# Nine matmuls behind the heads' products read their columns in other orders, by a word for each of fourteen units

## Chip, cores and metric

The kernel runs on one core of a Trainium2 chip. The metric is the device time of one execution in microseconds, the median of several runs. Before the change it is 1700.52 us (three runs, 1699.19 to 1701.03).

## What is computed

One decoder layer on 256 rows of 4096 float32 numbers: an RMS norm, a projection to q, k, v and gate of 32 heads, stick-breaking attention, a second projection that is added to the input, and a last RMS norm.

```python
xn = rms_norm(x, norm_attn)
q, k, v, g = split(xn @ w_in, 4)              # w_in: 4096 x 16384
# per head, strictly causal (s < t):
log_a[t, s] = log_sigmoid(z[t, s]) + sum_{s < j < t} log_sigmoid(-z[t, j]),  z = q k^T / sqrt(128)
o = exp(log_a) @ v
h = x + (o * silu(g)) @ w_out                 # w_out: 4096 x 4096
out = rms_norm(h, final_norm)
```

## The kernel before

**Arithmetic.** Both factors of a large product are split into a high part and a rest (`h` and `l`, both float32r), and a product is the sum of three matmuls: high by high, high by rest, rest by high. Each has 128 rows, 128 stationary columns and 512 moving columns, and adds into one PSUM bank. `mm3` (line 813) issues the three. The moving operand is a slice of a weight tile (`wh`, `wl`), the stationary one a block of the input (`sh`, `sl`; in the second projection `oh`, `ol`).

**Units.** The work is cut into 20 units: units 0 to 15 take the columns of `w_in` that give two heads each, units 16 to 19 the columns of `w_out`. A unit has 16 steps, each over 256 of the 4096 rows of the contraction. From unit 1 on, a step has seven or eight products (a Strassen form in some steps, the plain form with two shared sums in the others), so 21 or 24 matmuls. Seven PSUM banks gather a unit's products (`acc`), the eighth (`att`) serves the heads.

**Heads.** While the products of unit u run, the two heads of unit u-1 are worked off. Each head has four groups of small products on TensorE: the transposes (`tr`), the scores (`z`), the scan that sums the logs (`z` again) and the weighted values (`o`). So a unit u from 2 to 15 has eight such groups among its big products. `ten` (line 345) gives a group to the planner with an earlier key than any big product, so that it is next on TensorE as soon as its inputs are there.

**Who sets the order.** `Plan` is an event-driven planner with a cost for each instruction. It emits the instructions of all engines in one order. TensorE takes them in that order, ScalarE makes the high parts `wh`, VectorE the rests `wl` and, at a unit's end, adds up the banks (`combine`), SyncE loads the weights as `raw`, GpSimd issues loads that add.

**Order of reading.** A matmul's 512 columns may be read in any order, if the output is written in the same one. `mm3` rearranges both by two numbers q and e: the 512 columns are cut into pieces of q*e, and the matmul makes q rounds, in each of which it takes the next run of e columns from every piece. A letter names the order: `e` is 4 rounds in runs of 8, `c` is 4 rounds in runs of 4. A word of three letters belongs to a product, one letter to each of its matmuls. `product` (line 1234) chooses the word: `since_others` counts the big products since the last group of a head, and the first seven take the words of `BEHIND_OTHERS` (line 37): `ccc ecc eee eee eee eee cce`. Later the first product of a step takes one of `IN_STEP`, and every other product is `eee`.

Of the kernel before, what the change touches and what calls it, by code (L numbers as in the profile page):

```python
# [31 lines left out]
NS = KC // KT  # L32
EPS = 1e-6

ROUNDS = 4
RUNS = {"e": 8, "c": 4}
BEHIND_OTHERS = ("ccc", "ecc", "eee", "eee", "eee", "eee", "cce")
IN_STEP = ("cce", "ecc")
WARM, IDLE = 10, 640


# [207 lines left out]
def kernel(  # L249
# [61 lines left out]
    for g, (n, k) in enumerate(order):  # L311
        p = parts[n]
# [30 lines left out]
    since_others = 0  # L343
# [469 lines left out]
    def mm3(out_, a, b, start, stop, orders):  # L813

        (ah, al), (bh, bl) = a, b
        for k, (x, y) in enumerate(((ah, bh), (ah, bl), (al, bh))):
            to, y = (t.rearrange("p (h q e) -> p q h e", q=ROUNDS, e=RUNS[orders[k]]) for t in (out_, y))
            nc.tensor.matmul(to, x, y, start=start and k == 0, stop=stop and k == 2, skip_group_check=True)


# [413 lines left out]
    def product(n, k):  # L1234
        nonlocal since_others
        p = parts[n]
        b, f, c = p["prods"][k]
        h, l = forms[p["s"]]
        orders = "eee"
        if since_others < len(BEHIND_OTHERS):  # L1240
            orders = BEHIND_OTHERS[since_others]
        elif p["i"] == 0 and k == 0:
            orders = IN_STEP[p["s"] % len(IN_STEP)]
        since_others += 1
        mm3(
            ev[p["u"]][b],
            (h[:, PLACES[f], :], l[:, PLACES[f], :]),
            tuple(t[:, c].rearrange("p i n -> p (i n)") for t in (wh[n], wl[n])),
            starts[p["u"], b] == (n, k),
            ends[p["u"], b] == (n, k),  # L1250
            orders,
        )

    def products():
        for g, (n, k) in enumerate(order):
            p = parts[n]
            u, s = p["u"], p["s"]
            b, f, c = p["prods"][k]
            if u < 1:
                what = "s"  # L1260
            elif u < OUT0:
                what = "n"
            elif u == OUT0:
                what = "o"
            else:
                what = "r" if u == LAST and s in EIGHT_LAST else "p"
            if starts[u, b] == (n, k):
                yield nc.take(f"b{b}")
                ev.setdefault(u, {})[b] = acc.tile([P, W], F32, tag=f"b{b}", name=f"acc{u}_{b}")
            yield nc.until(("low", n, c), ("form", what, s), lead=nc.LEAD)  # L1270
            yield nc.work(
                "tensor", PRODUCT, lambda: product(n, k), g * PRODUCT, after=lambda n=n, k=k: done(n, k), hold=False
            )
            nc.here = g * PRODUCT
# [59 lines left out]
```

## Time and profile before

| | |
|---|---|
| median of three runs | 1700.52 us |
| the profiled execution | 1698.9 us |
| its span, first to last instruction | 1697.1 us |
| TensorE, granted clock | 0.997 |
| big matmuls, all units | 7158 |

The profiled execution is 1.8 us longer than its span, and 1.6 us shorter than the median. The profile names one line for every instruction, because all are recorded in one helper; tiles tell them apart. In the timeline each row has the start, the duration, the engine and the tiles (output<-operands); a matmul's duration is that of its whole way through the array, so it is the distance between two starts that tells how fast TensorE goes on.

### The profile page before, as it was taken

How to read it: one execution, taken by the hardware profiler on the slowest of the kernel's cores; microseconds unless marked ns; L12 is line 12 of the kernel's file. 1: busy time of each engine (PE TensorE's matmuls, PEld its weight loads, DVE VectorE, ACT ScalarE, POOL GpSimd, SP SyncE). 2: the span in 40 equal slices, each digit the busy share in tenths (PEclk: the TensorE clock that was granted, in tenths of full speed). 3: DMA queues.
4: the chain of work that ended last, by engine and by line, in shares of the span. 5: the costliest groups of instructions: out<-in, count | busy, mean ns of one | idle time of the engine just before them, and what ended most of it. 6: DMA issues, size and time to landing. Idle time of an engine off the chain costs nothing.

```text
span 1697.1 us, 25128 instructions
## 1 busy us (share of the span) xinstructions
PE 1680.2 (99%) x7776; PEld 1417.4 (84%) x7776; DVE 1602.0 (94%) x2025; ACT 1206.7 (71%) x1665; POOL 324.9 (19%) x400
## 2 busy tenths in 40 slices
PE   9999999999999999999999999999999999999997
PEld 7888888888888888888888888888888888888885
DVE  8899999999999999999999999999999978999997
ACT  8986767676767676767676767676868775656654
POOL 0012222121222222222212121212122111212110
PEclk9999999999999999999999999999999999999998
DMA  9978888878787878797978797979797978888895
GB/s 343 332 197 247 232 247 222 252 217 253 215 256 212 256 212 266 199 272 196 276 201 269 198 268 196 272 198 269 204 264 210 300 230 266 245 245 256 246 304 185
DMA packets 248438, 412.77 MB, mean 243 GB/s; under 512 B 28016, under 2 KB 72560, under 8 KB 248304
## 3 DMA queue, kind: packets, MB, share of 16 engines
q1 hardware_dynamic: 194544, 354.24, 62.7%
q0 software_dynamic: 53472, 56.65, 20.0%
q8 instruction: 61, 1.00, 0.2%
q14 instruction: 73, 0.60, 0.1%
q10 hardware_dynamic: 288, 0.28, 0.1%
HBM read 402.93 MB, written 8.13 MB: 242 GB/s over the span
## 4 chain that ended last, share of the span: by engine, by line
PE 94%; DVE 3%; DMA 1%; issue 1%; ACT 1%; SPq 0%; DVEq 0%; ACTq 0%
PE acc L132 89%; PE z L132 3%; PE o L132 1%; DVE wl L132 1%; PE tr L132 1%; DVE h L132 1%; DVE raw L132 0%; ACT wh L132 0%; DMA raw<-in_w_out_dram 0%; DMA raw<-in_w_in_dram 0%; DMA xres<-in_x_dram 0%; SPq L132 0%; ACT sq L132 0%; DVE scalars L132 0%; DVE qk_sb L132 0%
## 5 line engine op out<-in xcount | busy, mean ns | idle before, releaser
L132 ACT CAST wh<-raw 128x1024 fp32r<-128x1024 f32 (+1 forms) x989 | 919.3, 970 | 385.5 <-DVE raw L132 160.9
L132 DVE TENSOR_TENSOR wl<-raw,wh 128x1024 fp32r<-128x1024 f32 (+1 forms) x815 | 975.7, 1220 | 49.3 <-ACT wh L132 23.9
L132 PE MATMUL acc<-wh,sh 128*128 128x512 f32 x2048 | 771.9, 389 | 0.1
L132 PE MATMUL acc<-wh,sl 128*128 128x512 f32 x1898 | 727.1, 383 | 1.8 <-DVE sl L132 1.8
L132 PE MATMUL acc<-wl,sh 128*128 128x512 f32 x1748 | 668.9, 383 | 0.1
L132 PEld LDWEIGHTS acc<-wh,sh 128*128 128x128 f32 x2048 | 384.0, 188 | 77.9 <-DVE qk_sb L132 4.9
L132 POOL DMA_DIRECT2D raw<-in_w_in_dram x300 | 258.3, 947 | 972.2 <-DMA raw<-in_w_in_dram 375.1
L132 PEld LDWEIGHTS acc<-wh,sl 128*128 128x128 f32 x1898 | 356.0, 188 | 66.3 <-DVE sl L132 2.4
L132 PEld LDWEIGHTS acc<-wl,sh 128*128 128x128 f32 x1748 | 328.4, 188 | 55.6 <-DVE wl L132 0.4
L132 DVE TENSOR_TENSOR raw<-raw,raw 128x512 f32<-128x512 f32 x348 | 238.3, 688 | 15.3 <-DMA raw<-in_w_in_dram 11.7
L132 PE MATMUL acc<-wh,oh 128*128 128x512 f32 x512 | 192.4, 383 | 0.0
L132 PE MATMUL acc<-wh,ol 128*128 128x512 f32 x488 | 186.7, 383 | 0.0
L132 PE MATMUL acc<-wl,oh 128*128 128x512 f32 x464 | 177.6, 383 | 1.4 <-DVE wl L132 1.4
L132 DVE TENSOR_TENSOR wh<-raw,wh 128x512 fp32r<-128x512 f32 x174 | 119.7, 688 | 3.3 <-ACT wh L132 2.7
L132 DVE TENSOR_TENSOR raw<-raw 128x512 f32<-128x512 f32 x174 | 119.4, 686 | 0.0
L132 PEld LDWEIGHTS acc<-wh,oh 128*128 128x128 f32 x512 | 96.1, 188 | 17.3
L132 PEld LDWEIGHTS acc<-wh,ol 128*128 128x128 f32 x488 | 91.5, 188 | 16.1
L132 PEld LDWEIGHTS acc<-wl,oh 128*128 128x128 f32 x464 | 87.1, 188 | 17.6 <-DVE wl L132 2.2
L132 POOL DMA_DIRECT2D raw<-in_w_out_dram x48 | 41.5, 984 | 173.8 <-DMA raw<-in_w_out_dram 85.2
L132 ACT ACTIVATE f<-f 128x384 f32<-128x384 f32 x96 | 50.5, 526 | 3.0
L132 POOL DMA_DIRECT2D p<-spill x27 | 17.0, 676 | 89.9 <-DVE ol L132 32.0
L132 DVE SCALAR_TENSOR_TENSOR gv_sb<-acc,scalars,gv_sb 128x512 f32<-128x512 f32 x45 | 33.5, 745 | 0.0
(86 smaller groups left out, 765.7 us busy)
## 6 DMA issues: line engine op xcount, KB each, us to landing
raw<-in_w_in_dram SPq DMA_DIRECT2D x1024, 256.0 KB, 4.5
raw<-in_w_out_dram SPq DMA_DIRECT2D x256, 256.0 KB, 4.5
raw<-in_w_in_dram POOLq DMA_DIRECT2D x300, 128.0 KB, 5.2
p<-spill POOLq DMA_DIRECT2D x27, 256.0 KB, 4.6
raw<-in_w_out_dram POOLq DMA_DIRECT2D x48, 128.0 KB, 5.4
xr<-in_x_dram SPq DMA_DIRECT2D x16, 256.0 KB, 5.3
xres<-in_x_dram SPq DMA_DIRECT2D x16, 256.0 KB, 5.5
out_dram<-h SPq DMA_DIRECT2D x16, 256.0 KB, 2.8
```

The lines of the kernel that those rows point to most:

```text
L132: return self.tc.keep_in_program_order(getattr(self.engine, name)(*args, **kw))
```

## The change

Two more orders get a letter: `g` is 2 rounds in runs of 8, and `r` reads the 512 columns as they lie. In units 2 to 15 the first three products behind each group of a head take their three words from a table by unit, in place of `ccc ecc eee`; the fourth to seventh stay as they are, and so do all other units.

```diff
-ROUNDS = 4
-RUNS = {"e": 8, "c": 4}
+RUNS = {"e": (4, 8), "c": (4, 4), "g": (2, 8), "r": (1, 512)}
 BEHIND_OTHERS = ("ccc", "ecc", "eee", "eee", "eee", "eee", "cce")
 IN_STEP = ("cce", "ecc")
+BY_UNIT = (
+    "cec eee eee", "cce eee eee", "ecc eee eee", "cce ccc eee", "ecc ece eee", "gcc eee eee", "ece cec ccc",
+    "eee eec cee", "ece eee eee", "ccc cee eee", "eee eee eee", "ccr eee eee", "cec cec eee", "ecc ccc eee",
+)
...
-            to, y = (t.rearrange("p (h q e) -> p q h e", q=ROUNDS, e=RUNS[orders[k]]) for t in (out_, y))
+            q, e = RUNS[orders[k]]
+            to, y = (t.rearrange("p (h q e) -> p q h e", q=q, e=e) for t in (out_, y)) if q > 1 else (out_, y)
...
             orders = BEHIND_OTHERS[since_others]
+            if 2 <= p["u"] < 2 + len(BY_UNIT) and since_others < 3:
+                orders = BY_UNIT[p["u"] - 2].split()[since_others]
```

No instruction is added, removed or moved on any engine, and no wait changes. 384 of the 7158 big matmuls get another order: 296 go from `c` to `e`, 72 from `e` to `c`, 8 from `c` to `g` and 8 from `c` to `r`.

On TensorE in unit 12, behind the transposes of the second head of unit 11, there stood (128x4x32x4 is order `c`, 128x4x16x8 order `e`; the name behind the arrow is the moving tile, then the stationary one):

```order
L132 MATMUL tr11_1_10144<-ident_129,qk_sb11_9832 128x128 x4
L132 MATMUL acc12_3_9963<-wh617_10004,sh4_279 128x4x32x4 x2
L132 MATMUL acc12_3_9963<-wh617_10004,sl4_280 128x4x32x4
L132 MATMUL acc12_7_9998<-wh618_10034,sh4_279 128x4x16x8
L132 MATMUL acc12_7_9998<-wl618_10124,sh4_279 128x4x32x4
L132 MATMUL acc12_7_9998<-wh618_10034,sl4_280 128x4x32x4
L132 MATMUL acc12_5_9944<-wh618_10034,sh4_279 128x4x16x8
```

and now there stands, with the word `eee eee eee` of unit 12:

```order
L135 MATMUL tr11_1_10144<-ident_129,qk_sb11_9832 128x128 x4
L135 MATMUL acc12_3_9963<-wh617_10004,sh4_279 128x4x16x8 x2
L135 MATMUL acc12_3_9963<-wh617_10004,sl4_280 128x4x16x8
L135 MATMUL acc12_7_9998<-wh618_10034,sh4_279 128x4x16x8
L135 MATMUL acc12_7_9998<-wl618_10124,sh4_279 128x4x16x8
L135 MATMUL acc12_7_9998<-wh618_10034,sl4_280 128x4x16x8
L135 MATMUL acc12_5_9944<-wh618_10034,sh4_279 128x4x16x8
```

The same matmuls stand in the same places; all five that were in order `c` are in order `e`.

On TensorE in unit 8, behind the scores of the second head of unit 7, there stood:

```order
L132 MATMUL z7_1_6980<-off_139,ident_b_140 128x256
L132 MATMUL acc8_1_6777<-wh412_6865,sh5_325 128x4x32x4
L132 MATMUL acc8_1_6777<-wl412_6876,sh5_325 128x4x32x4
L132 MATMUL acc8_1_6777<-wh412_6865,sl5_326 128x4x32x4
L132 MATMUL acc8_2_6710<-wh412_6865,sh5_325 128x4x16x8
L132 MATMUL acc8_2_6710<-wl412_6876,sh5_325 128x4x32x4
L132 MATMUL acc8_2_6710<-wh412_6865,sl5_326 128x4x32x4
L132 MATMUL acc8_3_6759<-wh413_6850,sh5_325 128x4x16x8 x2
L132 MATMUL acc8_3_6759<-wh413_6850,sl5_326 128x4x16x8
```

and now, with the word `ece cec ccc` of unit 8:

```order
L135 MATMUL z7_1_6980<-off_139,ident_b_140 128x256
L135 MATMUL acc8_1_6777<-wh412_6865,sh5_325 128x4x16x8
L135 MATMUL acc8_1_6777<-wl412_6876,sh5_325 128x4x32x4
L135 MATMUL acc8_1_6777<-wh412_6865,sl5_326 128x4x16x8
L135 MATMUL acc8_2_6710<-wh412_6865,sh5_325 128x4x32x4
L135 MATMUL acc8_2_6710<-wl412_6876,sh5_325 128x4x16x8
L135 MATMUL acc8_2_6710<-wh412_6865,sl5_326 128x4x32x4
L135 MATMUL acc8_3_6759<-wh413_6850,sh5_325 128x4x32x4 x2
L135 MATMUL acc8_3_6759<-wh413_6850,sl5_326 128x4x32x4
```

Again only the orders differ: seven of the nine have changed, and the third product, which had none in order `c`, has all three.

## The prediction

> **What bounds the kernel now.** I read the page first: the busy time of each engine against the span.
>
> ```profile
> span 1697.1 us, 25128 instructions
> ...
> PE 1680.2 (99%) x7776; PEld 1417.4 (84%) x7776; DVE 1602.0 (94%) x2025; ACT 1206.7 (71%) x1665; POOL 324.9 (19%) x400
> ```
>
> TensorE is busy for 99% of the span, VectorE for 94%. Then one unit alone, from the table of stretches (length, then TensorE, weight loads, VectorE and so on):
>
> ```profile
> 599.00:683.00 84.00, 84.00 (x393) 70.94 (x393) 81.33 (x98) 61.12 (x81) 17.73 (x21) 1.00 0.83 235
> ```
>
> Within this steady unit TensorE has no gap, and its granted clock is 1.00. VectorE is busy for 81.33 of 84.00 us, so it could follow a TensorE that were 2.7 us faster in a unit. What TensorE does wait for, the list of waits shows:
>
> ```profile
> PEld acc L132 <- DVE qk_sb L132: 4.9, 14, 0.5
> PEld acc L132 <- PE acc L132: 4.7, 14, 0.3
> ```
>
> Each comes 14 times, once at each turn from one unit to the next: a bank of the old unit must be added up by VectorE before the new one may use it (the second row blames a matmul; the timeline has VectorE's `gv_sb` add ending there). Together they are (4.9 + 4.7) / 14 = 0.69 us for each unit. Apart from them a steady unit's time is the sum of the distances between starts on TensorE. The change touches nothing but the order in which 384 matmuls read, so it can act only through these distances, and I read them from the timeline of TensorE.
>
> **What the old words cost.** Behind the transposes of the second head in unit 6 (the first row holds the first two big matmuls, the second the tenth, the third the fifteenth):
>
> ```profile
> 537.89 0.69 PE L132 MATMUL acc<-wh,sh 128*128 128x512 f32 x2
> ...
> 539.98 0.38 PE L132 MATMUL acc<-wh,sh 128*128 128x512 f32 x1
> ...
> 541.08 0.38 PE L132 MATMUL acc<-wh,sl 128*128 128x512 f32 x1
> ```
>
> From the tenth to the fifteenth are five distances in 1.10 us: 0.220 us each. This is the quiet pace, in order `e`. From the first to the tenth are nine distances in 2.09 us, where the quiet pace would give 1.98: **0.11 us too long**. I call this the excess of a group. Behind the scores of the same head:
>
> ```profile
> 541.99 0.47 PE L132 MATMUL acc<-wh,sh 128*128 128x512 f32 x1
> ...
> 543.89 0.39 PE L132 MATMUL acc<-wh,sl 128*128 128x512 f32 x1
> 544.12 0.38 PE L132 MATMUL acc<-wh,sh 128*128 128x512 f32 x1
> ```
>
> Nine distances in 2.13 us: excess 0.15. The last of them, 0.23 us, is between two matmuls in order `e`, so the same order goes at two paces: the quiet one, and a slow one that an interruption leaves behind and that ends at some later point. Behind the scan and behind the values of that head (first and tenth matmul of each):
>
> ```profile
> 550.01 0.47 PE L132 MATMUL acc<-wh,sh 128*128 128x512 f32 x1
> ...
> 552.14 0.38 PE L132 MATMUL acc<-wh,sh 128*128 128x512 f32 x1
> ...
> 554.13 0.47 PE L132 MATMUL acc<-wh,sh 128*128 128x512 f32 x1
> ...
> 556.23 0.38 PE L132 MATMUL acc<-wh,sh 128*128 128x512 f32 x1
> ```
>
> The excesses are 0.15 and 0.12. The mean of the four is (0.11 + 0.15 + 0.15 + 0.12) / 4 = **0.13 us with `ccc ecc eee`**. I take it for seven of the eight groups of a unit; the first one is apart, below.
>
> **What words without a pair of `c` cost.** No group of a head is followed by another word in this trace, so I take the nearest rows: matmuls in order `e` behind another interruption, a wait. In unit 0 (interrupted matmul, the next one, and the tenth behind the wait's end):
>
> ```profile
> 10.12 0.50 PE L132 MATMUL acc<-wh,sl 128*128 128x512 f32 x1 [1.75 <-DVE sl L132]
> 10.45 0.40 PE L132 MATMUL acc<-wh,sh 128*128 128x512 f32 x1
> ...
> 12.53 0.40 PE L132 MATMUL acc<-wh,sh 128*128 128x512 f32 x1
> ```
>
> The restart itself takes 0.33 us, 0.11 too long. The nine distances behind it take 2.08 us, 0.10 too long, or 0.011 each, and the slow pace has not ended when the next `ccc` comes at 12.53. And in unit 17 (first and eleventh matmul behind a wait, all in order `e`):
>
> ```profile
> 1515.60 0.50 PE L132 MATMUL acc<-wl,oh 128*128 128x512 f32 x1 [0.29 <-DVE wl L132]
> ...
> 1518.07 0.39 PE L132 MATMUL acc<-wh,ol 128*128 128x512 f32 x1
> ```
>
> Ten distances in 2.47 us: 0.27 too long. So ten distances in order `e` cost 0.21 to 0.27, which I take as **0.24, or 0.11 more than the old words**. If the pace then stays slow until the seventh product's `cce`, up to nine more matmuls pay 0.011 each. From the starts above, the scores are followed by (550.01 - 541.99) / 0.22, over 30 matmuls, the scan by (554.13 - 550.01) / 0.22, under 19, so I add a mean of 0.06. An `e` word costs 0.11 + 0.06 = 0.17 us a group more, seven groups 1.2 us a unit. The ends are 0, if order `e` behind a group gets quiet as soon as the old words do, and 7 x (0.27 - 0.13 + 0.10) = 1.7 us.
>
> **What one pair of `c` costs.** In the first group of a unit the transposes are followed by one product, then the wait on VectorE of 0.3 us, then a product in `ecc` and one in `eee`, up to the scores. That is a pair of `c` behind an interruption with no second pair. In unit 6 (first matmul behind the wait, and the scores, six matmuls later):
>
> ```profile
> 516.52 0.47 PE L132 MATMUL acc<-wh,sh 128*128 128x512 f32 x1
> ...
> 517.97 0.82 PE L132 MATMUL z<-qkT 128*128 128x128 f32 x4
> ```
>
> and the same place in unit 7:
>
> ```profile
> 600.77 0.46 PE L132 MATMUL acc<-wh,sh 128*128 128x512 f32 x1
> ...
> 602.18 0.38 PE L132 MATMUL z<-qkT 128*128 128x128 f32 x2
> ```
>
> 1.45 and 1.41 us for six distances of 0.22 (1.32): excesses 0.13 and 0.09. In unit 7 the pair ended the slow pace, in unit 6 it did not (both last distances are rounded to 0.01). With four more matmuls, quiet or at 0.011, a group would have 0.09 or 0.17; the mean, 0.13, is that of the old words. So **one pair at the front is worth as much as the old two**, on the mean: 0 us, with 0.04 either way.
>
> **The sum.** Units by word:
> - A pair of `c` in the first product (units 3, 4, 5, 6, 7, 11, 13, 15): 0. This puts `gcc` and `ccr` with the others; `g` and `r` stand in no big matmul of this trace, and 16 matmuls are too few to matter unless they spoil the pair beside them, at most 7 x 0.17 = 1.2 us in each of the two units.
> - No two `c` side by side in all nine (units 2, 10, 12): `eee eee eee` 1.2 us. `cec` and `ece` hold single ones; between 0 and 1.2, I take the middle, 0.6 each. Together 2.4 us.
> - Two `c` side by side, but late: `cec cec` at the third and fourth matmul (unit 14), `ece cec ccc` at the sixth (unit 8), `eec cee` there too (unit 9). Until then each matmul pays 0.011 more: 7 x 0.02, 7 x 0.06 and 7 x 0.07, together 1.0 us.
> - The first group of each unit: its first product lies beside the wait on VectorE, which ends when VectorE is done, so a slower or faster word there costs nothing as long as the wait of 0.3 us is left. In the product behind the wait, `eee` takes the place of `ecc` in units 2, 3, 4, 7, 10, 12 and 13: 0.11 + 5 x 0.011 = 0.165 against the mean of 0.13 and 0.09, or 0.05 more, seven times: 0.4 us.
>
> 2.4 + 1.0 + 0.4 = **3.8 us longer**. The profiled execution of 1698.9 us would become 1702.7; the median was 1700.5, which gives **1704.3 us**. A difference of 0.2%, 3.4 us, is about what a measurement of this kernel can tell from no change, so the forecast lies just beyond it.
>
> **The rivals.**
> 1. *The orders settle nothing.* The slow pace ends by itself after a while, and pairs of `c` only shift when. Then words cost what they cost now: 1700.5, at most 1 us off. For it: in the rows behind the scores the pace is slow at the tenth matmul in spite of two pairs. Against it: at 10.45 it lasted nine matmuls without a `c` and more. The Trainium skill goes further in "TensorE: Matmul & The Clock Gate", section "Back-to-back issue gap": the gap depends on the number of columns alone, which for 512 warm columns is 216 ns. By that no word could cost anything, and the time would stay 1700.5. The trace does not agree: the same 512 columns go at 220 and at 230 ns.
> 2. *Faster: the second pair was waste.* If one pair always ends the slow pace, as in unit 7, a group falls from 0.13 to 0.09. In the eight units with a pair at the front that is 8 x 7 x 0.04 = 2.2 us; if the single `c` do as well, in all fourteen units 3.9 us: 1696.6 to 1698.3. It decides from the point at which more than nine in ten groups lock at the first pair; unit 6 speaks against that.
> 3. *Slower by much: only the old words lock.* Every new word behaves as order `e`: 14 x 1.2 = 16.8 us, 1717. If half of them do, 1709. Against it: unit 7.
> 4. *VectorE gives it back.* A unit that takes longer lets VectorE, with 2.7 us free, get ahead, and the 0.69 us of waiting at the turn shrinks. Then units 2, 10, 12 keep at most 0.5 us of their 1.2 and the sum is under 1 us: 1701.3. Against it is the row
>
> ```profile
> ACT wh L132 <- PE acc L132: 148.7, 106, 4.5
> ```
>
> ScalarE waits 106 times for TensorE to free a tile, and VectorE's rests come behind ScalarE's high parts, so both are mostly paced by TensorE and come later with it.
>
> **How the numbers follow.** Chances: the forecast, 2 to 7 us longer, 50%; rival 1, 17%; rival 2, 13%; rival 3 beyond 7 us, 10%; rival 4, 10%. The forecast's lower end, 2 to 3.4 us, is within 0.2% and has 8 of its 50; rival 2 reaches beyond -3.4 us only if nearly every group locks, 5 of its 13, and I add 1 for what I do not see. That gives faster 6%, same 42%, slower 52%. The range of 8 in 10 leaves out the far half of rival 2 and the far part of rival 3: from 1698.5 to 1709. Its upper end is half the bound of rival 3, its lower end half the bound of rival 2.
>
> **What would show it.** In the profile after, the same places by the same reading: in unit 12 nine distances behind a group take 2.2 us or more, in unit 2 and 10 between that and the old 2.11, in units 3, 4, 5, 15 some groups 2.07 and others 2.15, as before on the mean. The length of unit 12 should be about 1 us over that of unit 15. The two waits at the turn should still be 0.3 to 0.5 us; if they shrink, rival 4 holds. If unit 12 is as long as before, the price of order `e` behind a group was wrong, and with it the sum; if units 3 and 4 are the ones that grew, the pair at the front was. No other engine's work should change.

## The result and the profile after

The changed kernel takes **1704.86 us** (median of six runs, 1704.20 to 1706.13), the kernel before 1700.30 in as many: the ratio is 1.0033, with a 95% interval of 1.0023 to 1.0043. It is slower by 4.6 us, and the interval begins just above 0.2%.

The page after, again first the span and the busy times:

```profile
span 1702.9 us, 25128 instructions
...
PE 1686.2 (99%) x7776; PEld 1417.7 (83%) x7776; DVE 1604.1 (94%) x2025; ACT 1208.2 (71%) x1665; POOL 324.8 (19%) x400
```

The span is 5.8 us longer than before, TensorE is busy for 6.0 us more with the same instructions, and VectorE for 2.1. The longest of the fourteen units, unit 5, in the table of stretches:

```profile
431.20:516.10 84.90, 84.90 (x393) 71.03 (x393) 81.43 (x98) 61.11 (x83) 17.38 (x22) 1.00 0.83 232
```

TensorE is still without a gap and its granted clock is still 1.00, so the added 0.8 us of this unit is in the distances between matmuls. The waits at the turn of a unit are in sum as they were (4.9 and 4.7 before):

```profile
PEld acc L135 <- DVE qk_sb L135: 4.8, 14, 0.4
PEld acc L135 <- PE acc L135: 4.7, 14, 0.3
```

Unit 6 again, with the word `ecc ece eee`: first and tenth matmul behind the transposes, the scores, the scan and the values of the second head, and of the last group the twenty-second too:

```profile
541.02 0.47 PE L135 MATMUL acc<-wh,sh 128*128 128x512 f32 x1
...
543.13 0.39 PE L135 MATMUL acc<-wh,sh 128*128 128x512 f32 x1
...
545.19 0.47 PE L135 MATMUL acc<-wh,sh 128*128 128x512 f32 x1
...
547.29 0.38 PE L135 MATMUL acc<-wh,sh 128*128 128x512 f32 x1
...
553.17 0.48 PE L135 MATMUL acc<-wh,sh 128*128 128x512 f32 x1
...
555.33 0.39 PE L135 MATMUL acc<-wh,sh 128*128 128x512 f32 x1
...
557.39 0.47 PE L135 MATMUL acc<-wh,sh 128*128 128x512 f32 x1
...
559.53 0.39 PE L135 MATMUL acc<-wh,sh 128*128 128x512 f32 x1
...
562.28 0.39 PE L135 MATMUL acc<-wh,sh 128*128 128x512 f32 x1
```

The excesses over nine quiet distances (1.98) are 0.13, 0.12, 0.18 and 0.16; before they were 0.11, 0.15, 0.15 and 0.12. That is only 0.06 more in all. The last two rows show where more is lost: from the tenth to the twenty-second matmul are twelve distances in 2.75 us, where twelve quiet ones take 2.64. Before, the same stretch (556.23 to the row below) took 2.64:

```profile
558.87 0.38 PE L132 MATMUL acc<-wh,sh 128*128 128x512 f32 x1
```

Lined up matmul by matmul, the two traces give each unit's length, from its first big matmul to that of the next unit. The differences, with the prices that the prediction put on the words (what it put on the first groups, 0.05 in seven units, is not in the column):

| unit | word | priced | after - before, us |
|---|---|---|---|
| 2 | cec eee eee | 0.6 | +0.48 |
| 3 | cce eee eee | 0 | +0.78 |
| 4 | ecc eee eee | 0 | +0.39 |
| 5 | cce ccc eee | 0 | +0.84 |
| 6 | ecc ece eee | 0 | +0.45 |
| 7 | gcc eee eee | 0 | -0.22 |
| 8 | ece cec ccc | 0.4 | +0.30 |
| 9 | eee eec cee | 0.5 | -0.02 |
| 10 | ece eee eee | 0.6 | +0.51 |
| 11 | ccc cee eee | 0 | +0.36 |
| 12 | eee eee eee | 1.2 | +0.61 |
| 13 | ccr eee eee | 0 | +0.29 |
| 14 | cec cec eee | 0.1 | +0.13 |
| 15 | ecc ccc eee | 0 | +0.23 |

Together +5.13 us. By place behind a group: +0.79 us in the first nine distances, **+3.95 in the tenth to the twenty-first**, +0.39 later. So three quarters are lost among matmuls whose order did not change. The rest of the 5.8 us lies where no word changed: the first big matmul starts 0.75 us later in its trace than before, unit 0 is 0.22 shorter, and units 16 to 19 are together 0.09 longer (17 is 0.29 shorter, 18 0.61 longer).

Two rows of the table are not the words' alone. At the turn into unit 7 the profile before has a longer wait than at any other turn:

```profile
598.76 0.19 PEld L132 LDWEIGHTS acc<-wh,sh 128*128 128x128 f32 x1 [0.50 <-DVE qk_sb L132]
```

From the last matmul ahead of it to this start are 0.47 us; in the change it is 0.31, as at the other turns before. So 0.17 of the 0.22 us that unit 7 gained are a shorter wait, and `gcc` itself gained 0.05. All differences of unit 7 below have this 0.17 us in them. In unit 8 of the change the wait is the longer one, by 0.09 us.

A count of groups shows the mechanism. Take the seven groups behind the first of each of the fourteen units, 98 in all, and call a group still slow if the two distances behind its tenth matmul are together more than 8 ns too long. Before, 0 of 98 are still slow; in the change 55 are, 33 of them among the 56 groups with a pair at the front.

### The profile page after: what moved, and what is told of

It reads as the page before. It is cut to its first block, busy times and chain, and to the rows that moved or that the text cites. A ratio compares the mean times of both kernels' runs of the same rounds, so it can differ in the third digit from the quotient of the medians.

```text
span 1702.9 us, 25128 instructions
## 1 busy us (share of the span) xinstructions
PE 1686.2 (99%) x7776; PEld 1417.7 (83%) x7776; DVE 1604.1 (94%) x2025; ACT 1208.2 (71%) x1665; POOL 324.8 (19%) x400
```

## The experiments

Each kernel keeps everything but the table of words and, where a diff shows it, how the table is read; the diffs are against the changed kernel and leave out the old table. Ratios are against the kernel before, run on the same chip. "By the traces" is the sum over units 2 to 15 of one profiled execution, less that of the profile before.

**The same words elsewhere.**

```diff
 BY_UNIT = (
+    "ece cec ccc", "eee eec cee", "ece eee eee", "ccc cee eee", "eee eee eee", "ccr eee eee", "cec cec eee",
+    "ecc ccc eee", "cec eee eee", "cce eee eee", "ecc eee eee", "cce ccc eee", "ecc ece eee", "gcc eee eee",
 )
```

> The fourteen words of the change, each moved on by seven units (the word of unit 2 to unit 9, that of unit 7 to unit 14, that of unit 9 to unit 2). If a word has its price wherever it stands, the whole takes 4 to 5 us more than the kernel before, as the change does; unit 14, now with gcc, is at most 84.0 us long, unit 2, now with eee eec cee, within 0.05 us of its old 84.09, and units 10 and 12 (cce eee eee, cce ccc eee) 0.7 to 0.9 us longer than before. If the price belongs to the unit (its state at the turn, its place in the kernel), units 3 and 5 stay the long ones and unit 7 the short one.

The table was in fact moved by eight units, not seven: `gcc` stands in unit 15, `eee eec cee` in unit 3, `cce eee eee` in 11, `cce ccc eee` in 13. Measured: ratio 1.0042 (1.0029 to 1.0056), and by the traces +5.12 us in the fourteen units, as in the change. Half of the words, seven of the fourteen, took their prices along within 0.1 us (in brackets the price in the change): `gcc` -0.17 (-0.22), `eee eec cee` +0.02 (-0.02), `cce eee eee` +0.73 (+0.78), `cce ccc eee` +0.75 (+0.84), `ecc eee eee` +0.35 (+0.39), `ecc ece eee` +0.45 (+0.45), `ece cec ccc` +0.33 (+0.30). For `gcc` that is in part chance, since its -0.22 was mostly the wait. Units 3 and 5 are not the long ones any more. The other seven moved by 0.11 us or more: `eee eee eee` fell from +0.61 to +0.03, `cec cec eee` rose from +0.13 to +0.65. So a price belongs in part to the word, and in part to something else; what the unit is entered with is the likely one, but this run alone does not show it.

**Order e alone.**

```diff
+BY_UNIT = ("eee eee eee",) * 14
```

> All fourteen units with eee eee eee. The price put on it in the prediction was 1.2 us a unit: 16.8 us more than the kernel before, 1717. What unit 12 showed in the change is 0.61 us: 14 times that is 8.5 us, 1709. If the slow pace ended by itself as soon as with the old words: 1700.

Measured: ratio 1.0045 (1.0030 to 1.0060), 8.1 us between the medians; by the traces 9.83 us in the fourteen units, 0.55 to 0.82 each (the 0.55 is unit 7). The 16.8 us of the prediction is refuted, the 8.5 us from unit 12 holds. The values of the second head in unit 10 of this kernel (first, tenth, twenty-second matmul):

```profile
896.09 0.47 PE L132 MATMUL acc<-wh,sh 128*128 128x512 f32 x1
...
898.22 0.39 PE L132 MATMUL acc<-wh,sh 128*128 128x512 f32 x1
...
900.98 0.39 PE L132 MATMUL acc<-wh,sh 128*128 128x512 f32 x1
```

2.13 us for the first nine distances, only 0.03 more than `ccc ecc eee` in the same place (2.10), and 2.76 for the next twelve, 0.12 more. Order `e` is hardly dearer at the front, but the slow pace goes on: 85 of the 98 groups are still slow behind the tenth matmul. The other 13 got quiet without any `c`; they are the scores of the first head in units 3 to 15.

**The word that had gained, in all units.**

```diff
+BY_UNIT = ("gcc eee eee",) * 14
```

> All fourteen units with gcc eee eee. If the word has its price wherever it stands, 14 x (84.00 - 84.22) = 3 us less than the kernel before: 1697.2, within 1 us. If unit 7 was luck of its place, the same as the other words with a pair at the front, 0.4 to 0.8 us a unit more: 1706 to 1711. The prediction put it at 0: 1700.5.

Measured: ratio 1.0006 (0.9997 to 1.0015), no gain; by the traces +1.46 us in the fourteen units. The 3 us of the first expectation took the shorter wait of unit 7 for the word's. In unit 10, the scores of the second head and then its values (first, tenth, twenty-second of each):

```profile
878.82 0.48 PE L132 MATMUL acc<-wh,sh 128*128 128x512 f32 x1
...
880.97 0.40 PE L132 MATMUL acc<-wh,sh 128*128 128x512 f32 x1
...
883.74 0.38 PE L132 MATMUL acc<-wh,sh 128*128 128x512 f32 x1
...
891.07 0.48 PE L132 MATMUL acc<-wh,sh 128*128 128x512 f32 x1
...
893.14 0.38 PE L132 MATMUL acc<-wh,sh 128*128 128x512 f32 x1
...
895.78 0.38 PE L132 MATMUL acc<-wh,sh 128*128 128x512 f32 x1
```

Behind the values 2.07 and 2.64 us: a quick start, and quiet afterwards. Behind the scores 2.15 and 2.77: the slow pace goes on. In unit 7 of the change the scores of the second head had been quiet from the fourth matmul on; in a row of units with `gcc` they are not. 29 of the 98 groups are still slow behind the tenth matmul, two in each unit and a third in unit 5.

**Each order by itself.** Every product of units 2 to 4 and 14, 15 in `e`, of 5 to 7 in `c`, of 8 to 10 in `g`, of 11 to 13 in `r`.

```diff
+BY_UNIT = ("eee", "eee", "eee", "ccc", "ccc", "ccc", "ggg", "ggg", "ggg", "rrr", "rrr", "rrr", "eee", "eee")
...
+        if 2 <= p["u"] < 2 + len(BY_UNIT):
+            orders = BY_UNIT[p["u"] - 2]
```

> Every product of units 2 to 4 in order e, of 5 to 7 in c, of 8 to 10 in g, of 11 to 13 in r, of 14 and 15 in e; no words behind the heads or at steps in these units. For the pace of each order where nothing interrupts it. Theory: the quiet pace of 0.220 us is the pace of the array and the same for all four; what differs is only whether a pace that was made slow gets quiet again, so units in e, without any c, stay slow for long (0.6 us or more over 84.09). Rival: the orders have paces of their own, c and r slower than e by over 2 ns a matmul, which would be 0.7 us or more a unit.

One run: 1724.0 us. Behind the values of the second head, from the tenth to the twenty-second matmul, in unit 6 (`c`), unit 9 (`g`), unit 12 (`r`) and unit 15 (`e`):

```profile
561.44 0.38 PE L132 MATMUL acc<-wh,sh 128*128 128x512 f32 x1
...
564.17 0.39 PE L132 MATMUL acc<-wh,sh 128*128 128x512 f32 x1
...
821.10 0.40 PE L132 MATMUL acc<-wh,sh 128*128 128x512 f32 x1
...
823.90 0.40 PE L132 MATMUL acc<-wh,sh 128*128 128x512 f32 x1
...
1081.69 0.39 PE L132 MATMUL acc<-wh,sh 128*128 128x512 f32 x1
...
1084.41 0.39 PE L132 MATMUL acc<-wh,sh 128*128 128x512 f32 x1
...
1337.68 0.38 PE L132 MATMUL acc<-wh,sh 128*128 128x512 f32 x1
...
1340.32 0.38 PE L132 MATMUL acc<-wh,sh 128*128 128x512 f32 x1
```

Twelve distances in 2.73, 2.80, 2.72 and 2.64 us: 0.227, 0.233, 0.227 and 0.220 us each. The rival holds: the orders have paces of their own, and `e`, when quiet, has the best. `c`, `g` and `r` keep these paces for some 190 matmuls behind the last group of a unit. The Trainium skill, "Advanced Engine Details and Errata", section "Memory Cachelines", says of PSUM that any pattern that is not contiguous slows matmuls significantly; here the contiguous order `r` is 3% slower than runs of eight, and the measurement decides.

What the theory said of `e` holds for four of the five units in `e`, which took 0.62 us or more longer; unit 14 took 0.17. Unit 3 took 2.42 us longer, since there the slow pace did not end: behind the values of its second head, from the sixtieth to the hundred and tenth matmul,

```profile
316.36 0.39 PE L132 MATMUL acc<-wh,sl 128*128 128x512 f32 x1
...
327.90 0.39 PE L132 MATMUL acc<-wl,sh 128*128 128x512 f32 x1
```

are fifty distances in 11.54 us, 0.231 us each, where the quiet pace gives 11.00. It goes on like this to the end of the unit, while in the other four units this stretch is quiet. So in `e` the pace can be quiet without any `c`, and a slow one can last for some 190 matmuls.

**One late pair.**

```diff
+BY_UNIT = ("eee eec cee",) * 14
```

> All fourteen units with eee eec cee: no pair of c in the first five matmuls behind a group, one pair at the sixth and seventh. Theory: what counts is not how the first nine begin but that the slow pace is ended before the tenth, and a pair that comes after five matmuls in e always ends it (seven of seven groups in unit 9 of the change). Then all units are within 0.05 us of the kernel before, 14 x (84.07 - 84.09) = 0 us, 1699 to 1700. Rival: a pair at the front is what counts, as the prediction had it: 7 x 0.06 to 0.07 us a unit more, 1705 to 1706.

Measured: ratio 1.0007 (0.9998 to 1.0016); by the traces +1.37 us. The rival's 5 to 6 us is refuted, and a front without any pair is nearly as good as the old words. But "always" is too much: nine units are between -0.10 and +0.08 us, five between +0.21 and +0.27, and 23 of the 98 groups are still slow behind the tenth matmul.

**Fourteen other words, in two places.**

```diff
+BY_UNIT = (
+    "gcc eee cce", "gcc eec cee", "gcc cce eee", "gcc ecc eee", "gec cee eee", "ccc eec cee", "ccc eee cce",
+    "ccc cce eee", "eec cee eee", "eee cce eee", "eee ecc eee", "ecc eec cee", "gcc eee eee cce", "gce eec cee",
+)
...
-            if 2 <= p["u"] < 2 + len(BY_UNIT) and since_others < 3:
+            if 2 <= p["u"] < 2 + len(BY_UNIT) and since_others < len(BY_UNIT[p["u"] - 2].split()):
```

> Fourteen other words in units 2 to 15, in this order: gcc eee cce, gcc eec cee, gcc cce eee, gcc ecc eee, gec cee eee, ccc eec cee, ccc eee cce, ccc cce eee, eec cee eee, eee cce eee, eee ecc eee, ecc eec cee, gcc eee eee cce, gce eec cee. Theory: a word with a pair of c between the fifth and the ninth matmul leaves under 0.1 us a unit behind the ninth, with whatever front, and is within 0.15 us of the unit before; with gcc in front 0.1 to 0.3 us shorter. Rival (every word is luck of the entry): units spread over -0.2 to +0.8 us, as in the change, with no regard to the pair's place.

> The same fourteen words, each five units earlier (the word of unit 7 in unit 2, that of unit 2 in unit 11). If a word has its price wherever it stands, each is within 0.1 us of what it gave in the other place; if the entry decides, not.

One run of each: 1701.1 and 1701.4 us; +2.47 and +2.93 us in the fourteen units. Eight of the fourteen words are within 0.1 us of themselves in the other place. `ccc eee cce` (-0.01 and -0.11) and `eee cce eee` (-0.04 and -0.07) are below the old words both times. `ecc eec cee` has its pair where the theory wants it and yet loses 0.41 and 0.34; `gec cee eee` goes from +0.05 to +0.43. So the pair's place alone does not tell, and the first theory is wrong in that.

**Two words in turn, and the best one alone.**

```diff
+BY_UNIT = ("ccc eee cce", "gcc eee eee") * 7
```

> ccc eee cce in units 2, 4, ... 14 and gcc eee eee in units 3, 5, ... 15. gcc alone among other words made its unit 0.17 and 0.22 us shorter, but fourteen of them in a row 0.08 to 0.13 us longer each. If that is the entry (what the unit before leaves), gcc behind another word is 0.2 us shorter again and ccc eee cce 0.01 to 0.11 shorter: 7 x (-0.2) + 7 x (-0.06) = -1.8 us, 1697. If not, 7 x 0.1 - 7 x 0.06 = +0.3 us, 1699.

Measured: ratio 0.9996 (0.9987 to 1.0005); by the traces -0.39 us, between the two expectations: the `gcc` units lie between -0.13 and +0.14. 11 of the 98 groups are still slow behind the tenth matmul.

```diff
+BY_UNIT = ("ccc eee cce",) * 14
```

> All fourteen units with ccc eee cce, which took -0.01 and -0.11 us in its two units: if the price holds in a row, 14 x (-0.06) = -0.8 us against the kernel before; if a row of one word finds an entry of its own, as gcc did, up to +0.1 us a unit, +1.4 us.

Measured: ratio 0.9996 (0.9987 to 1.0005); by the traces -0.73 us, near the -0.8 of a price that holds, though 0.17 of it are the wait of unit 7. The scores of the second head in unit 10:

```profile
877.88 0.47 PE L132 MATMUL acc<-wh,sh 128*128 128x512 f32 x1
...
880.00 0.38 PE L132 MATMUL acc<-wh,sh 128*128 128x512 f32 x1
...
882.66 0.38 PE L132 MATMUL acc<-wh,sh 128*128 128x512 f32 x1
```

2.12 us to the tenth matmul (2.13 before), then 2.66, nearly quiet. None of the 98 groups is still slow behind the tenth matmul, as before. Neither version can be told from the kernel before by its time.

**Pairs behind the changed words.**

```diff
-            if 2 <= p["u"] < 2 + len(BY_UNIT) and since_others < 3:
-                orders = BY_UNIT[p["u"] - 2].split()[since_others]
+            if 2 <= p["u"] < 2 + len(BY_UNIT) and since_others < 5:
+                orders = (BY_UNIT[p["u"] - 2].split() + ["cce", "ecc"])[since_others]
```

> The change's own fourteen words, and behind them cce and ecc in place of eee eee for the fourth and fifth product. In the change 3.95 of the 5.13 us that units 2 to 15 lost lie between the tenth and the twenty-first matmul behind a group. Theory: that is the slow pace, which lasts because no pair ends it; the two pairs end it, at a price of 0.01 to 0.04 us each, so that under 2 us of the 3.95 are left and the units lose 2 to 3.5 us in all: 1701.5 to 1703. Rival: these matmuls are late for another reason (weights, VectorE); then the pairs change nothing or add their price, 5 to 7 us, 1704 to 1706.

Measured: ratio 1.0031 (1.0019 to 1.0042); by the traces +5.03 us, nearly as much as the change. My theory that any pair ends the slow pace falls here. The number is the rival's, but its reason (weights, VectorE) does not fit the other experiments: with the same loads and the same work on VectorE, the words alone leave 0 groups still slow or 85. The single groups show why the pairs did not help. Excess of each distance in ns over 220, with the letter of its matmul, behind a scan in unit 12 and in unit 9 of the change, and behind the values of the first head in unit 3 of this kernel:

```
unit 12:  e94 e10 e17 | e7  e9  e10 | e10 e17 e8  | e9  e10 e11
unit  9:  e94 e10 e17 | e8  e9  c14 | c19 e5  e1  | e-1 e1  e0
unit  3:  c92 c3  e12 | e9  e16 e3  | e10 e10 e16 | c14 c7  e8  | e9
```

The slow pace of order `e` is a cycle of five distances: 10, 10, 17, 7 and 9 ns too long. In unit 9 the pair comes behind 17-8-9 and ends it; in unit 3 it comes behind 10-10-16 and does not. I counted the pairs of `c` behind three distances of this cycle, in the traces of before, of the change and of all experiments but the one with whole units:

| the three distances ahead of the pair | ended at once | not |
|---|---|---|
| 17, 7, 9 | 40 | 0 |
| 9, 10, 10 | 17 | 0 |
| 7, 9, 10 | 0 | 54 |
| 10, 10, 17 | 0 | 29 |
| 10, 17, 7 | 0 | 46 |

(Each reading is good to 1 ns; 16 counts as 17, 8 as 7, 10, 10, 10 as 9, 10, 10, and 7, 10, 10 as 7, 9, 10. A pair counts if one more matmul in `e`, not the first of its group, stands ahead of the three, and two more big matmuls follow the pair.) A pair ends the slow pace at two of the five places of the cycle and never at the other three.

Pairs behind other slow distances are not in the table. Most of them stand behind `ccc eee`, where the three distances are about 8, 9 and 13 ns too long: 74 pairs, 43 of them in the experiment with `ccc eee cce` in all units, and all 74 ended the slow pace. Behind 13, 6 and 8, none of 14 did. The pace ahead of a group counts as well. Behind the values of a unit's first head, where the first five matmuls are in `e`, the pace was quiet from the second on in all 15 groups with three quiet distances ahead, and slow in all 17 with three distances of 5 ns or more too long. So what a word costs hangs on how many matmuls lie between the interruption and its pair, and on the pace at which the stream is interrupted. What in TensorE goes round in five steps, and why a pair ends it, was not tried.

## Why the prediction held, and where it did not

**What bounds the kernel: right.** TensorE has no gap in a unit, no other engine's work changed, the waits at the turn differ by the 0.17 us in unit 7, the 0.09 in unit 8 and 0.03 or less elsewhere, and the time went where the prediction looked for it, into the distances between matmuls. Rival 4 (VectorE gives it back) is out: the waits at the turn are 4.8 and 4.7 us, before 4.9 and 4.7.

**The total: right by luck, from terms that are wrong.** The prediction had 3.8 us; the fourteen units took 5.13 by the traces, the medians 4.6. By its own classes:

- *A pair at the front, eight units: 0 was predicted, 3.12 us came.* This is the step that failed. It said: "With four more matmuls, quiet or at 0.011, a group would have 0.09 or 0.17". It stopped at the tenth matmul, while it let the words in `e` pay for up to nine matmuls more. Where the pair had not ended the slow pace, those nine pay as well: of the 5.13 us, 3.95 lie there. With the same 0.06 us that it added for `e`, for half of seven groups, it would have had 0.2 us a unit; the units took 0.4 on the mean. In fact 33 of the 56 groups were still slow behind the tenth matmul, and none with the old words: one pair at the front was not worth as much as the old two.
- *No pair, units 2, 10 and 12: 2.4 predicted, 1.60 came.* Of the 0.17 us a group, the 0.06 behind the tenth matmul was right: with order `e` alone it was 0.06 (0.43 us a unit in seven groups). The 0.11 in the first nine was not: it was 0.03 (0.21 us a unit). Both rows it was taken from, matmuls behind a wait, are dearer than matmuls behind a group: 0.21 and 0.27 for ten distances against 0.18. (The row at 12.53 begins a `cce`, not a `ccc`; the reading does not hang on it.)
- *A late pair, units 8, 9 and 14: 1.0 predicted, 0.41 came.* The price of a slow first five matmuls was taken at 0.011 each over the old words. In unit 9 the first nine distances of the seven groups came to 0.01 us less than before, since three of the seven began quiet in `e` and the old words are not quiet there either.
- *The first group of a unit: 0.4 predicted; in its first nine distances it came to -0.04 over all units.* The wait on VectorE hid the first product, as was said.

**The rivals.** Rival 1 (the orders settle nothing) is refuted by order `e` alone, 8 us longer, and by the words that kept their prices in other units (`cce ccc eee` +0.84 and +0.75). So is the gap by the number of columns alone (the Trainium skill, "TensorE: Matmul & The Clock Gate", section "Back-to-back issue gap", which calls it the gap of a single matmul in isolation): the same 512 columns went at 220, 227 and 233 ns. Rival 2 (faster) came true in single units with `gcc` (-0.17 in unit 15 of the first experiment), and not when all units had it. Rival 3 put 1.2 us on each unit; no unit reached 0.9.

**The tests it named.** Nine distances behind a group in unit 12 were to take 2.2 us or more: in the seven groups they took 2.07 to 2.16. Unit 12 was to be about 1 us longer than unit 15: it was 0.38. Units 3, 4, 5 and 15 were to stay as before on the mean: 3 and 5 grew most. The prediction named that sign as its own refutation of the pair at the front, and it came.

## What to carry to other kernels

When a stream of matmuls is interrupted, read the distances between starts far behind the interruption, not only where the order was changed: most of the loss was in matmuls that had not been touched. A price read over a short stretch must be carried on to the point where the state ends, for every case alike. And a forecast of a sum should be checked by its parts, since here two wrong terms, 3.1 us too little and 1.8 too much, gave a total within 1.3 us.

## What the runs showed of the hardware

- The same matmul of 512 float32r columns goes at 0.220, 0.227 or 0.233 us by the order in which the columns are read, and at 0.231 in the slow pace of order `e` (220 plus a fifth of 53 ns).
- An interruption of the stream often leaves a state that lasts over dozens of matmuls: with order `e` alone it was ended in some groups only by a pair of `c` at the nineteenth matmul or later, and in one unit without any `c` it lasted for some 190 matmuls.
- A pair of `c` ends the cycle of order `e` at two of its five places (57 of 57 pairs) and not at the other three (0 of 129).
- The state repeats: with `eee eee eee` in a row of units, units 3 to 15 were 84.767 us long within 1 ns.
